# A hybrid attention layer on one core: every attention stage gets its own place in the order, and the second attention's values take one matmul per key block

## The chip, the cores and the metric

The kernel runs on one core of one Trainium2 chip. Its engines work side by side, each through its own queue: TensorE (PE; its weight loads are listed as PEld) multiplies matrices into banks of PSUM, VectorE (DVE) and ScalarE (ACT) work element by element, GpSimd (POOL) does a few scalings, and SyncE (SP) issues most transfers. An engine takes its instructions in their order, and one that waits holds up all that stand behind it. The metric is the time of one execution in microseconds; lower is better.

## The reference

One decoder layer on 256 tokens of width 1024, in 32-bit floats. The normalised input is multiplied by one wide matrix, and the result is cut into the inputs of three mixers and their gates:

```python
h = rmsnorm(x, g_in);  z = h @ w_in
(mq, mk, mv, mg, dq, dk, dv, dg, iq, ik, iw, xq, xg, glog) = split(z)
ya = moba_attention(rope(mq), rope(mk), mv)              # 8 heads of 64
yb = dsa_attention(rope(dq), rope(dk), dv, rope(iq), rope(ik), iw)   # 8 heads, the 64 best keys each
yc = cross_attention(xq, *split(rmsnorm(mem, g_mem) @ w_mem_kv))     # 4 heads of 128, 256 memory rows
u  = sum over b of sigmoid(glog_b + b_merge_b) * ((y_b * silu(gate_b)) @ w_up_b)
out = rmsnorm(x + u @ w_out, g_final)
```

With 256 tokens the first attention (m) has one block, its own, and is plain causal attention. The second (d) adds a selection mask: an indexer scores all keys for each query from iq, ik and iw, and the 64 best stay.

## The kernel before

**Precision in halves.** A matrix product of 32-bit numbers is taken as three products of rounded parts: a number is split into hi (rounded) and lo (the rest), and hi·hi, hi·lo and lo·hi are added up in PSUM. So each weight piece (w0, w1, … in the order of use) is loaded raw (w5r), cast to hi on ScalarE (w5h, L253) and subtracted to lo on VectorE (w5l, L255), two operations of 128x1024 for most pieces, and then used by TensorE three times. The token activations (x) and the memory rows (e) are split the same way once.

**Steps.** The program is a list of numbered steps, each one weight piece; a step has two halves of 12 matmuls for most products. ORDER gives the sequence of the products: mq, mk, i (the indexer), dq, dk, xq (cross queries), xk and xv (cross keys and values), the gates mg, dg and xg, then l (the merge gates' logits), u (the up projections) and at the end the output. Everything else is attached by step number: `at(25.5, f)` runs f between the two halves of step 25, `at(26, f)` before its first half. Weights are loaded six steps ahead and split three steps ahead.

**Who sets the order.** TensorE and GpSimd run in the order in which the program is written, that is, by these steps. The order on VectorE, ScalarE and SyncE is set by the framework's scheduler from when it thinks operands are ready; LO_BEHIND pins one weight's subtraction behind one value split.

**Attention stages.** One block of the first or second attention is a pair of heads. `scores` puts both heads' scores (msc or dsc, six matmuls a head) into one PSUM bank each, tag "sc", of which there are two. VectorE reduces each with mask and maximum (L608, shown as CUSTOM_DVE and a read of its accumulator), ScalarE takes the exponentials with their sums (L612), VectorE the reciprocal (L620), GpSimd scales (mpr, dpr, L622), TensorE transposes (mtp, dtp, one bank, tag "tp", L633), ScalarE casts hi (L634), VectorE subtracts lo (mpl, dpl, L635), TensorE multiplies by the values (mya, dya, L648), and ScalarE and VectorE bring the result out (L653, L654). A value operand carries hi and lo of v side by side in its 128 columns, so that rows 0 to 63 of the product are hi and 64 to 127 lo. Four matmuls make a head: probabilities hi and lo, for each of two key blocks (256 and 128 query columns). They go into one half of the bank of tag "y" (there is one), the pair of heads shares the bank, and one copy (ScalarE) and one add (VectorE) bring a head out.

The indexer's queries and keys are rotated (the rope products, L408 to L412), split (iqs, iks), transposed through the "sc" banks (iqt, L459) and the "tp" bank (ikt, L463); its heads' scores (lg, L486) take "sc" banks too. The cross attention takes "sc" for its scores (xsc) and "y" for its values (xya). mBt (L919) spreads the memory rows' scale m_rstd.

M_PAIRS, D_PAIRS and X_HEADS give two steps for each pair or head, from which `attend` derives the other stages by fixed distances.

Of the kernel before, what the change touches and what calls it, by code (L numbers as in the profile page):

```python
# [68 lines left out]
)  # L69
# [43 lines left out]
def hybrid_layer_kernel(  # L113
# [144 lines left out]
    def product(ps, a, b, first, last):  # L258
        (ah, al), (bh, bl) = a, b
        nc.tensor.matmul(ps, ah, bh, start=first, stop=False)  # L260
# [1 line left out]
        nc.tensor.matmul(ps, al, bh, start=False, stop=last)  # L262
# [812 lines left out]
```

## Time and profile before

| | us |
|---|---|
| time, median of 3 runs | 323.35 (322.94 to 323.82) |
| span of the profiled execution | 321.2 |
| TensorE busy | 313.0 (97%) |
| TensorE weight loads busy | 298.2 (93%) |
| VectorE busy | 252.1 (78%) |
| ScalarE busy | 202.4 (63%) |
| GpSimd busy | 42.1 (13%) |
| TensorE clock granted, mean | 0.994 |

The profiled execution shows its span, from its first to its last instruction, and no time of its own beside it; 323.35 − 321.2 = 2.15 us is what lies around the span if it ran like the median. Busy time is a share of the span; matmuls overlap in the pipeline, so a busy TensorE may still be running at less than its best. The chain that ended last is followed back from the last instruction, and shows which engine had to be faster for the end to come earlier. A row of the timeline gives start, duration, engine, line, operation and operands (out<-in); what a row waited for is in brackets.

### The profile page before, as it was taken

The numbers are of one execution on the slowest core, as the hardware profiler recorded it, in microseconds if no ns is written. First come the engines' busy times: TensorE is split into PE (matmuls) and PEld (weight loads), VectorE is DVE, ScalarE is ACT, GpSimd is POOL, SyncE is SP. The second block draws the span as 40 slices with busy tenths as digits, with TensorE's granted clock in tenths as the row PEclk, the third lists the DMA queues.
The fourth block names the chain that finished last, engine by engine and source line by source line (L and its number), as shares of the span: only waits on it lengthen the run. The fifth ranks groups of instructions, "written<-read, shape, count | busy, mean of one in ns | idle before, by whom it ended". The sixth has DMA issues, their size and how long they took to land.

```text
span 321.2 us, 6394 instructions
## 1 busy us (share of the span) xinstructions
PE 313.0 (97%) x2442; PEld 298.2 (93%) x2442; DVE 252.1 (78%) x458; ACT 202.4 (63%) x357; POOL 42.1 (13%) x58
## 2 busy tenths in 40 slices
PE   8999999999999999999999999999999999999992
PEld 7899999998999989889999999999999999998882
DVE  3579999999799999988866669999466866677533
ACT  5599665687877636477666688755454546653434
POOL 0001000017202000020200235411000111014011
PEclk9999999999999999999999999999999999999997
DMA  7999886965545346484444434488756666656003
GB/s 214 376 334 326 267 264 183 282 222 138 191 131 141 126 137 229 158 254 138 134 133 131 135 130 133 134 261 271 221 178 193 192 192 198 185 157 187 2 0 131
DMA packets 18367, 59.45 MB, mean 185 GB/s; under 512 B 2208, under 2 KB 2464, under 8 KB 18336
## 3 DMA queue, kind: packets, MB, share of 16 engines
q1 hardware_dynamic: 17760, 57.73, 57.3%
q10 hardware_dynamic: 576, 1.31, 1.1%
q8 instruction: 19, 0.31, 0.4%
q14 instruction: 12, 0.10, 0.1%
HBM read 55.89 MB, written 1.05 MB: 177 GB/s over the span
## 4 chain that ended last, share of the span: by engine, by line
PE 83%; ACT 5%; DVE 5%; DMA 3%; issue 2%; SPq 0%; ACTq 0%; DVEq 0%
DMA w3r<-w_in 2%; PE i_0ps L286 2%; PE i_1ps L286 2%; PE xv_0ps L286 2%; PE dv_0ps L286 2%; PE xv_1ps L286 2%; PE dv_1ps L286 2%; PE lg L486 1%; PE o_0ps L261 1%; PE o_0ps L262 1%; PE o_0ps L260 1%; DMA w0r<-w_in 1%; ACT mpr L612 1%; PE dya L648 1%; PE mv_1ps L286 1%
## 5 line engine op out<-in xcount | busy, mean ns | idle before, releaser
L753 POOL TENSOR_TENSOR u<-u,gt 128x512 f32<-128x512 f32 x7 | 9.9, 1413 | 76.7 <-DVE gt L750 76.7
L622 POOL TENSOR_SCALAR dpr<-dpr,dst 128x128 f32<-128x128 f32 (+1 forms) x16 | 6.6, 426 | 83.4 <-DVE dst L620 83.2
L622 POOL TENSOR_SCALAR mpr<-mpr,mst 128x128 f32<-128x128 f32 (+1 forms) x16 | 9.8, 628 | 56.0 <-DVE mst L620 56.0
L740 ACT ACTIVATE gt<-gt,x_first 128x256 f32<-128x256 f32 x24 | 10.9, 501 | 3.7 <-DVE gt L737 3.6
L612 ACT ACTIVATE dpr<-dms,dst 128x128 f32<-128x128 f32 (+1 forms) x16 | 7.1, 445 | 3.6 <-DVE dst L608 3.6
L612 ACT ACTIVATE mpr<-mms,mst 128x128 f32<-128x128 f32 (+1 forms) x16 | 7.1, 445 | 2.1 <-DVE mst L608 2.1
L794 ACT ACTIVATE junk<-xn 128x512 f32<-128x512 f32 (+1 forms) x5 | 2.7, 543 | 8.6 <-DVE xn L792 8.6
L670 ACT ACTIVATE xpr<-xsc,xst,xs_rstd 128x256 f32<-128x256 f32 x8 | 4.5, 560 | 4.1 <-DVE xst L666 4.1
L758 ACT CAST us<-u 128x512 fp32r<-128x512 f32 x4 | 2.5, 623 | 6.2 <-POOL u L753 4.9
L490 ACT ACTIVATE rl<-lg 128x384 f32<-128x384 f32 x8 | 3.9, 486 | 2.7 <-PE lg L486 1.6
L653 ACT COPY dyT<-dya 64x256 f32<-64x256 f32 x8 | 2.9, 368 | 4.2 <-PE dya L648 4.0
L493 DVE SCALAR_TENSOR_TENSOR acc<-rl,iw,acc 128x128 f32<-128x128 f32 (+1 forms) x14 | 5.4, 433 | 0.1
L974 PE MATMUL warm<-ones 128*128 128x128 f32 x18 | 4.2, 430 | 1.1 <-DVE eps_t L969 1.1
L486 PE MATMUL lg<-ikT,iqT 128*128 128x128 f32 (+1 forms) x32 | 5.1, 281 | 0.1
L608 DVE CUSTOM_DVE_ANT_0 mms<-msc,bias_c 128x128 f32<-128x128 f32 (+1 forms) x16 | 5.0, 348 | 0.0
L974 PEld LDWEIGHTS warm<-ones 128*128 128x128 f32 x18 | 3.9, 330 | 1.0 <-DVE eps_t L969 1.0
L635 DVE TENSOR_TENSOR dpl<-dtp,dph 128x384 fp32r<-128x384 f32 x8 | 4.4, 555 | 0.4
L654 DVE TENSOR_TENSOR dyT<-dyT,dya 64x256 f32<-64x256 f32 x8 | 3.3, 418 | 1.8 <-ACT dyT L653 1.7
L608 DVE CUSTOM_DVE_ANT_0 dms<-dsc,sel 128x128 f32<-128x128 f32 (+1 forms) x16 | 4.7, 353 | 0.0
L634 ACT CAST dph<-dtp 128x384 fp32r<-128x384 f32 x8 | 3.8, 479 | 1.4 <-PE dtp L633 1.3
L504 DVE MATCH_REPLACE8 wk<-m,wk 128x128 f32<-128x128 f32 (+1 forms) x14 | 4.7, 345 | 0.0
L792 DVE TENSOR_TENSOR xn<-o_0ps,xn 128x512 f32<-128x512 f32 x2 | 1.4, 692 | 4.2 <-PE o_0ps L262 4.2
(1296 smaller groups left out, 1544.3 us busy)
## 6 DMA issues: line engine op xcount, KB each, us to landing
x_rows<-x SPq DMA_DIRECT2D x2, 512.0 KB, 8.9
eT<-memT SPq DMA_DIRECT2D x4, 256.0 KB, 4.6
xn<-x SPq DMA_DIRECT2D x2, 512.0 KB, 4.8
w0r<-w_in SPq DMA_DIRECT2D x2, 256.0 KB, 3.3
w1r<-w_in SPq DMA_DIRECT2D x2, 256.0 KB, 4.3
xT<-xT SPq DMA_DIRECT2D x2, 256.0 KB, 6.6
w2r<-w_in SPq DMA_DIRECT2D x1, 512.0 KB, 6.7
w3r<-w_in ACTq DMA_DIRECT2D x1, 512.0 KB, 7.8
```

Source lines behind the costliest of these rows:

```text
L286: nc.tensor.matmul(accs[nm][t][:, :n], a[p](k, slice(t * P, (t + 1) * P)), w[q][:, half, :], start=k + i == 0, stop=k + i == nk + 1,)
L486: nc.tensor.matmul(lg[:, c : c + n], q[:, q0:q1], idx["k"][:, j, 0:n], start=j == 0, stop=j == 1)
L493: nc.vector.scalar_tensor_tensor(acc[:, c], rl[:, c], iw[:, t, g : g + 1], (bias_c if g == 0 else acc)[:, c], op0=OP.mult, op1=OP.add,)
L504: nc.vector.match_replace(out=wk[:, c], in_to_replace=m8[t], in_values=src[:, c], imm_value=TAKEN)
L608: nc.vector.tensor_tensor_reduce(out=ms[:, c], in0=sc[:, c], in1=bias()[:, c], op0=OP.add, op1=OP.min, scale=-(HD**-0.5), scalar=3e38, acc ...
L612: big["last_exp"] = nc.scalar.activation(pr[:, c], ms[:, c], AF.Exp, bias=st[:, t : t + 1], scale=-1.0, accum_out=st[:, 2 + t : 3 + t],)
L622: nc.gpsimd.tensor_scalar(pr[:, c], pr[:, c], st[:, 4 + t : 5 + t], 1.0, op0=OP.mult, op1=OP.mult)
L635: marks[f"{nm}pl{hd}"] = nc.vector.tensor_sub(pl, tp[:, 0 : 3 * P], ph.bitcast(F32)).ins
L670: big["last_exp"] = nc.scalar.activation(pr3[:, t, :], sc[:, t, :], AF.Exp, bias=st[:, t : t + 1], scale=xs_rstd[:, t : t + 1], accum_out= ...
L740: nc.scalar.activation(gt[:, f, :], gt[:, f, :], AF.Sigmoid, bias=x_first[:, j : j + 1])
L753: adder.tensor_tensor(u, u, gt, op=OP.add)
L974: nc.tensor.matmul(warm[:, 0:P], ones, ones, start=True, stop=True)
```

## The change

1. **Places.** The tables of pairs become one table per stage (scores, scales, turns, values), with an entry for every block or head, and the indexer's turn and heads, the ropes, and the memory rows get places of their own. ORDER is permuted. LO_BEHIND is empty.
2. **Second attention's values (APART).** hi and lo of a head's probabilities lie side by side in one tile; a head takes two matmuls, one per key block, with both halves as moving operand (512 columns, then two times 128 columns). Each head fills a whole "y" bank: [hi·hi and hi·lo | lo·hi and lo·lo]. One ScalarE copy and two VectorE adds bring three of these four quarters out.
3. **Shared banks.** The two column halves of mq, and of xk, share one PSUM bank; their evacuation is one operation where it was two. The indexer's keys are transposed into one tile and copied once.
4. **Tiles.** The reduction writes straight into the probabilities' tile (no ms); six such tiles in place of four.

SC, MM, SQ_ONE, EARLY and the branch for two blocks at once are new names whose values leave the work as it was.

```diff
-ORDER = (
-    "mk0", "mk1", "i0", "dq0", "xq0", "i1", "dq1", "dk0", "dk1", "xk0", "xq1", "dv", "xk1",
-    "xv", "mg0", "mg1", "dg0", "dg1", "xg0", "xg1", "l10", "l01", "l00", "u00", "l02", "u10",
-    "l20", "l03", "u01", "u02", "l21", "u03", "u20", "l11", "u11", "l22", "l23", "u21", "l12",
-    "l13", "u12", "u13", "u23", "u22",
-)
+ORDER = ('mk0', 'mk1', 'i0', 'xq0', 'dq0', 'i1', 'dq1', 'dk0', 'xq1', 'dk1', 'xk0', 'dv', 'xk1',
+         'xv', 'mg0', 'mg1', 'xg1', 'dg1', 'dg0', 'l01', 'xg0', 'l00', 'l10', 'u00', 'l02', 'u10',
+         'l20', 'l03', 'u01', 'u03', 'u20', 'l21', 'u02', 'l22', 'l11', 'l12', 'l23', 'u11', 'u21',
+         'l13', 'u12', 'u13', 'u23', 'u22')
...
-IDX = (27, 29, 33.5)
-TURNS = (('mq', 8.5, 15.5), ('mk', 13.5, 20.5), ('dq', 27, 30), ('dk', 34, 37.5))
-M_PAIRS = ((23, 25.5), (24, 27.5), (26.5, 29.5), (29.5, 31.5))
-D_PAIRS = ((43.5, 47.5), (47.5, 49), (52, 53.5), (54.5, 55.5))
-X_HEADS = ((41.5, 44), (44.5, 46.5), (49, 51), (50.5, 52.5))
+IDX_TURN = (27, 28, 28)
+IDX_HEADS = (29, 30.0, 30.0, 31.0, 31, 31.5, 32, 32.5)
+IDX_TOP = 33.5
+TURNS = (('mq', 8.5, 15.0), ('mk', 14.5, 20.5), ('dq', 28.0, 32.5), ('dk', 34, 35.5))
...
+M_BLOCKS = (1, 1, 1, 1)
+M_SCORES = (23, 25.5, 26.0, 29.5)
+M_SCALES = (23.5, 24.5, 27.0, 26.0, 27.0, 27.0, 30.0, 31.0)
+M_TURNS = (25.5, 26.5, 27.5, 28.5, 29.5, 30.5, 31.5, 33.5)
+M_VALUES = (26.5, 27.5, 28.5, 29.5, 30.5, 32.5, 34.0, 36.0)
+D_BLOCKS = (1, 1, 1, 1)
+D_SCORES = (43.5, 47.5, 52, 54.5)
+D_SCALES = (44, 44.5, 48, 48.5, 52.5, 53.5, 55, 56.5)
+D_TURNS = (45.5, 47.5, 49, 50, 53.5, 55.0, 56.0, 57.0)
+D_VALUES = (48.5, 49.0, 50, 51, 54.5, 56.0, 57.0, 61.0)
+X_SCORES = (41.5, 44.0, 48.5, 48.0)
+X_SCALES = (42, 45, 49.0, 51)
+X_TURNS = (44, 46.5, 51.0, 52.0)
+X_VALUES = (45.5, 48, 53.0, 53.5)
+MEM_ROWS = 23.5
+APART = ('d',)
 GATES = 59.5
-LO_BEHIND = {29: "mpl0"}
-MEM = (2, 7, 11, 15, 21.5)
+LO_BEHIND = {}
+MEM = (2, 3, 10, 15, 19.5)
...
+    def pair_bank(nm):
+        return acc_bank(nm).rearrange("p (f s) -> p f s", f=2)
...
+    def products_t(ps, w, act, ks, nk, cols, f=None):
...
-                (a[0](k, slice(0, S)), a[1](k, slice(0, S))), k == 0, k == nk - 1,
+                (a[0](k, slice(0, S)), a[1](k, slice(0, S))), k == 0 and not f, k == nk - 1,
+                f is not None,
...
-        tp = psum.tile([P, 2, S], F32R, name=f"ikt{t}", tag="tp", bufs=1)
-        for j in range(2):
-            nc.tensor.transpose(tp[:, j, 0:P], idx["ks", t][:, j, :], ident_r)
-        nc.vector.tensor_copy(idx["k"][:, :, tok], tp[:, :, 0:P])
+
+    def idx_keys():
+        tp = psum.tile([P, 2, S], F32R, name="ikt", tag="tp", bufs=1)
+        for u in range(2):
+            for j in range(2):
+                nc.tensor.transpose(tp[:, j, u * P : u * P + P], idx["ks", u][:, j, :], ident_r)
+        nc.vector.tensor_copy(idx["k"], tp)
...
-        for f in range(2):
-            nc.vector.tensor_tensor(sk[:, f, :], accs[f"xk{hf}"][f], mB, op=OP.mult)
+        nc.vector.tensor_tensor(sk, accs[f"xk{hf}"], pair_rows(mB), op=OP.mult)
...
-            ms = work.tile([P, 3 * P], F32, name=f"{nm}ms{hd}", tag="ms")
-            st = work.tile([P, 6], F32, name=f"{nm}st{hd}", tag="st", bufs=4)
-            pr = work.tile([P, 4 * P], F32, name=f"{nm}pr{hd}", tag="pr", bufs=4)
+            st = keep.tile([P, 6], F32, name=f"{nm}st{hd}", tag="st", bufs=6)
+            pr = work.tile([P, 4 * P], F32, name=f"{nm}pr{hd}", tag="pr", bufs=6)
...
-                    out=ms[:, c], in0=sc[:, c], in1=bias()[:, c], op0=OP.add, op1=OP.min,
+                    out=pr[:, c], in0=sc, in1=bias()[:, c], op0=OP.add, op1=OP.min,
...
     def self_values(nm, hd):
...
+        if nm in APART:
+            ya = psum.tile([P, 2, S], F32, name=f"{nm}ya{hd}", tag="y", bufs=1)
+            both = big[nm, "pt", hd]
+            nc.tensor.matmul(ya, v[:, 0, hd, :, :], both[:, :, 0:S], start=True, stop=False)
+            nc.tensor.matmul(
+                ya[:, :, P:S], v[:, 1, hd, :, :], both[:, :, S : 3 * P], start=False, stop=True
+            )
+            high, low = ya[0:HD], ya[HD:P]
+            if e:
+                first = keep.tile([P, S], F32, name=f"{nm}yf{hd}", tag="yf")[0:HD]
+                nc.scalar.copy(first, high[:, 0, :])
+                nc.vector.tensor_tensor(y, first, high[:, 1, :], op=OP.add)
+                nc.vector.tensor_tensor(y, y, low[:, 0, :], op=OP.add)
+            else:
+                nc.scalar.copy(y, low[:, 0, :])
+                for i in range(2):
+                    nc.vector.tensor_tensor(y, y, high[:, i, :], op=OP.add)
+            return
```

The first place is VectorE around the second score block of the first attention (mms or mpr on the left; msc_965 and msc_966 are its two heads before, msc_1008 and msc_1009 with the change; ISA is the masked reduction and the read of its accumulator). Before:

```order
L608 ISA mms_979,mst_980<-msc_965,bias_c 128x128
L608 ISA mst_980 128x1
L412 TENSOR_TENSOR ik_948<-ik1t_949,ik1t_950 128x64
L442 TENSOR_TENSOR iqs_954<-iq_648,iqs_954 128x8x64
L608 ISA mms_979,mst_980<-msc_965,bias_c 128x256
L608 ISA mst_980 128x1
L444 TENSOR_TENSOR iks_955<-ik_948,iks_955 128x64
L608 ISA mms_986,mst_987<-msc_966,bias_c 128x128
L608 ISA mst_987 128x1
L608 ISA mms_986,mst_987<-msc_966,bias_c 128x256
L608 ISA mst_987 128x1
L255 TENSOR_TENSOR w28l<-w28r,w28h 128x1024
```

and with the change:

```order
L656 RECIPROCAL mst_887<-mst_887 128x2
L275 TENSOR_TENSOR w28l<-w28r,w28h 128x1024
L437 TENSOR_TENSOR ik_942<-ik1t_943,ik1t_944 128x64
L467 TENSOR_TENSOR iqs_948<-iq_648,iqs_948 128x8x64
L469 TENSOR_TENSOR iks_949<-ik_942,iks_949 128x64
L644 ISA mpr_1023,mst_1022<-msc_1008,bias_c 128x128
L644 ISA mst_1022 128x1
L644 ISA mpr_1023,mst_1022<-msc_1008,bias_c 128x256
L644 ISA mst_1022 128x1
L644 ISA mpr_1029,mst_1028<-msc_1009,bias_c 128x128
L644 ISA mst_1028 128x1
L644 ISA mpr_1029,mst_1028<-msc_1009,bias_c 128x256
```

The weight split w28l and the rotated indexer halves (iqs, iks) now stand ahead of both reductions, where before the reductions stood between them and ahead of w28l. On TensorE the third block's scores come 12 product matmuls and one transposition behind the second's, where before 60 product matmuls, two transpositions and a head's values lay between.

The second place is TensorE at the first head of the second attention's values. Before:

```order
L648 MATMUL dya_2199<-dph_2118,dv 128x256
L648 MATMUL dya_2199<-dpl_2119,dv 128x256
L648 MATMUL dya_2199<-dph_2118,dv 128x128
L648 MATMUL dya_2199<-dpl_2119,dv 128x128
L633 MATMUL dtp_2208<-cst,dpr_1940 128x128 x3
L260 MATMUL dg0ps<-xhi,w48h 128x256
```

and with the change:

```order
L684 MATMUL dya_2188<-dpt_2009,dv 128x512
L685 MATMUL dya_2188<-dpt_2009,dv 128x2x128
L280 MATMUL xsc_2197<-xkh,xqT 128x256
L281 MATMUL xsc_2197<-xkl,xqT 128x256
L282 MATMUL xsc_2197<-xkh,xqT 128x256
L280 MATMUL xsc_2197<-xkh,xqT 128x256
L281 MATMUL xsc_2197<-xkl,xqT 128x256
L282 MATMUL xsc_2197<-xkh,xqT 128x256
```

Two matmuls stand for four, the second one with two strided pieces of 128 columns, and a head of cross scores now follows; 12 product matmuls later comes the second head.

The third place is VectorE at the same head (dyT is the result, dyf the odd heads' first quarter, xst the cross scores' maximum). Before:

```order
L709 COPY yxT<-xya_2169 128x256
L255 TENSOR_TENSOR w52l<-w52r,w52h 128x1024
L654 TENSOR_TENSOR dyT<-dyT,dya_2199 64x256
L635 TENSOR_TENSOR dpl_2207<-dtp_2208,dph_2206 128x384
L255 TENSOR_TENSOR w53l<-w53r,w53h 128x1024
L635 TENSOR_TENSOR dpl_2230<-dtp_2231,dph_2229 128x384
L665 TENSOR_REDUCE xst_2244<-xsc_2237 128x2
L666 TENSOR_TENSOR xst_2244<-xst_2244,xs_rstd 128x2
L654 TENSOR_TENSOR dyT<-dyT,dya_2199 64x256
```

and with the change:

```order
L719 TENSOR_REDUCE xst_2160<-xsc_2153 128x2
L275 TENSOR_TENSOR w52l<-w52r,w52h 128x1024
L720 TENSOR_TENSOR xst_2160<-xst_2160,xs_rstd 128x2
L697 TENSOR_TENSOR dyT<-dyT,dya_2188 64x256
L719 TENSOR_REDUCE xst_2204<-xsc_2197 128x2
L697 TENSOR_TENSOR dyT<-dyT,dya_2188 64x256
L720 TENSOR_TENSOR xst_2204<-xst_2204,xs_rstd 128x2
L732 RECIPROCAL xst_2160<-xst_2160 128x2
L732 RECIPROCAL xst_2204<-xst_2204 128x2
L692 TENSOR_TENSOR dyT<-dyf_2225,dya_2222 64x256
```

Each head has two adds, and the maximum of the next cross head stands between those of the first.

More of the change, by code (lines that the diff above doesn't have):

```diff
@@ L207, in row_sums @@
         ps = psum.tile([P, 512], F32, name=f"{nm}ss", tag="tp", bufs=1)
+        sq = acts[nm, "sq"]
+        if SQ_ONE:
+            nc.vector.tensor_tensor(sq[:, 0, :], sq[:, 0, :], sq[:, 1, :], op=OP.add)
         for t in range(2):
-            for j in range(2):
+            for j in range(2 - SQ_ONE):
                 nc.tensor.matmul(
-                    ps[:, t : t + 1], acts[nm, "sq"][:, j, t * P : (t + 1) * P], ones[:, 0:1],
-                    start=j == 0, stop=j == 1,
+                    ps[:, t : t + 1], sq[:, j, t * P : (t + 1) * P], ones[:, 0:1],
+                    start=j == 0, stop=SQ_ONE or j == 1,
                 )
@@ L456, in idx_transpose @@
         for j in range(2):
-            tp = psum.tile([P, 4, P], F32R, name=f"iqt{t}{j}", tag="sc", bufs=2)
+            tp = psum.tile([P, 4, P], F32R, name=f"iqt{t}{j}", tag="sc", bufs=SC)
             for g in range(4):
@@ L481, in idx_head @@
     def idx_head(g):
[L482 removed]
+        lg = psum.tile([P, 512], F32, name=f"lg{g}", tag="sc", bufs=SC)
         q = idx["q"][g // 4][:, g % 4, :]
@@ L488, in idx_head @@
                 )
-        rl = work.tile([P, 3 * P], F32, name=f"rl{g}", tag="ms")
+        rl = work.tile([P, 4 * P], F32, name=f"rl{g}", tag="pr", bufs=6)[:, 0 : 3 * P]
         nc.scalar.activation(rl, lg[:, : 3 * P], AF.Relu, scale=HD**-0.5)
@@ L499, in idx_round @@
         src, wk = idx["acc" if r == 0 else "wk"], idx["wk"]
-        m8 = [work.tile([P, 8], F32, name=f"m8_{r}{t}", tag="m8", bufs=4) for t in range(2)]
+        m8 = [
+            work.tile([P, 16], F32, name=f"m8_{r}{t}", tag="m8", bufs=4)[:, 0:8] for t in range(2)
+        ]
         for t, c in PARTS:
@@ L627, in self_transpose @@
         pr, _ = prs.pop((nm, hd))
-        ph, pl = prs[nm, "t", hd] = [
-            work.tile([P, 3 * P], F32R, name=f"{nm}p{p}{hd}", tag=f"pt{p}") for p in "hl"
-        ]
+        both = big[nm, "pt", hd] = work.tile([P, 2, 3 * P], F32R, name=f"{nm}pt{hd}", tag="pt")
+        ph, pl = prs[nm, "t", hd] = both[:, 0], both[:, 1]
         tp = psum.tile([P, 512], F32, name=f"{nm}tp{hd}", tag="tp", bufs=1)
@@ L650, in self_values @@
                 )
-        own, other = (slice(HD * i, HD * i + HD) for i in (e, 1 - e))
-        y = big[nm + "y"][own, b, :]
         nc.scalar.copy(y, ya[other, :])
@@ L658, in cross_scores @@
     def cross_scores(hd):
-        sc = psum.tile([P, 2, S], F32, name=f"xsc{hd}", tag="sc", bufs=2)
+        sc = psum.tile([P, 2, S], F32, name=f"xsc{hd}", tag="sc", bufs=SC)
         kT = [p[:, hd, :] for p in big["xk"]]
@@ L878, in hybrid_layer_kernel, with attend @@
     at(end["dv"], v_evac, "dv")
[L880 to L889 removed]
+    def attend(nm, blocks, starts, scales, turns, values, bias):
+        for g, s0 in enumerate(starts):
+            at(s0, self_scores, nm, sum(blocks[:g]), blocks[g], bias)
+        for hd in range(NH):
+            at(scales[hd], self_scale, nm, hd)
+            at(turns[hd], self_transpose, nm, hd)
+            at(values[hd], self_values, nm, hd)
+    attend("m", M_BLOCKS, M_SCORES, M_SCALES, M_TURNS, M_VALUES, lambda: bias_c)
+    attend("d", D_BLOCKS, D_SCORES, D_SCALES, D_TURNS, D_VALUES, lambda: idx["sel"])
     x_rows = []
```

138 lines of the change are left out of this document (70 added, 68 removed).

## The prediction

> **What bounds the kernel now.** I read the page first, then the chain, the waits of TensorE, the windows, and last the timeline of TensorE in the windows that are not full.
>
> ```profile
> span 321.2 us, 6394 instructions
> PE 313.0 (97%) x2442; PEld 298.2 (93%) x2442; DVE 252.1 (78%) x458; ACT 202.4 (63%) x357; POOL 42.1 (13%) x58
> ...
> PE 83%; ACT 5%; DVE 5%; DMA 3%; issue 2%; SPq 0%; ACTq 0%; DVEq 0%
> ```
>
> TensorE is busy for 313.0 of 321.2 us and the chain runs through it for 83% of the span. So an edit is worth what it takes from TensorE's own instructions, or from the few places where TensorE waits. The windows (PE, PEld, DVE, ACT, POOL, then clock, DMA, GB/s) show where these are:
>
> ```profile
> 60.00:70.00 10.00, 9.96 (x84) 9.07 (x83) 9.97 (x30) 8.99 (x17) 0.83 (x2) 1.00 0.83 266
> 70.00:80.00 10.00, 9.64 (x83) 8.80 (x82) 9.84 (x34) 7.08 (x21) 6.42 (x10) 1.00 0.51 143
> 80.00:90.00 10.00, 9.76 (x87) 9.62 (x87) 7.68 (x13) 7.93 (x18) 1.65 (x4) 1.00 0.62 184
> 90.00:100.00 10.00, 9.88 (x89) 9.37 (x88) 9.48 (x24) 8.28 (x21) 1.82 (x4) 1.00 0.36 109
> ...
> 190.00:200.00 10.00, 9.88 (x85) 9.68 (x84) 9.06 (x15) 8.54 (x16) 5.36 (x3) 1.00 0.49 152
> ```
>
> TensorE has gaps between 60 and 100 us and around 192 us. In 60 to 80 us VectorE is full (9.97 and 9.84 of 10), so anything that TensorE wants from VectorE there stands in a queue with no slack. The granted clock is 1.00 in all of these windows. The waits view and the starts on TensorE give the sizes (start, duration, line, operation):
>
> ```profile
> PE iqt L459 <- DVE mst L608: 0.4, 1, 0.4
> PE mq_0ps L262 <- DVE w3l L255: 0.2, 1, 0.2
> PE ikt L463 <- DVE mpl L635: 0.2, 1, 0.2
> ```
>
> ```profile
> 65.50 0.31 PE L286 MATMUL i_1ps<-w23h,xlo 128*128 128x320 f32 x1
> 65.85 0.40 PE L919 MATMUL mBt<-cst,m_rstd 128*128 128x128 f32 x2
> ...
> 67.06 0.33 PE L476 MATMUL msc<-mkhi,mqhi 64*128 64x128 f32 x2
> ...
> 67.95 0.39 PE L260 MATMUL dq1ps<-xhi,w24h 128*128 128x256 f32 x1
> ...
> 75.44 0.28 PE L648 MATMUL mya<-mph,mv 128*128 128x256 f32 x1
> 75.71 0.39 PE L648 MATMUL mya<-mpl,mv 128*128 128x256 f32 x1
> ...
> 77.90 0.28 PE L260 MATMUL dk0ps<-xhi,w26h 128*128 128x256 f32 x1
> ...
> 78.83 0.28 PE L262 MATMUL dk0ps<-xhi,w26l 128*128 128x256 f32 x1
> 79.47 1.10 PE L459 MATMUL iqt<-ident_r,iqs 128*128 128x128 f32 x8 [0.36 <-DVE mst L608]
> ...
> 84.22 0.80 PE L459 MATMUL iqt<-ident_r,iqs 128*128 128x128 f32 x8
> 85.23 0.36 PE L463 MATMUL ikt<-ident_r,iks 128*128 128x128 f32 x2 [0.21 <-DVE mpl L635]
> ...
> 94.53 0.28 PE L262 MATMUL dk1ps<-xhi,w29l 128*128 128x256 f32 x1
> 94.93 0.73 PE L486 MATMUL lg<-ikT,iqT 128*128 128x128 f32 x4
> ...
> 191.51 0.28 PE L648 MATMUL dya<-dph,dv 128*128 128x256 f32 x1
> 191.91 0.39 PE L648 MATMUL dya<-dpl,dv 128*128 128x256 f32 x1
> ```
>
> Durations overlap, so a wait shows in the starts. From 77.90 to 78.83 eight matmuls of 256 columns go by: 0.116 us each, the undisturbed pace. A start that comes later than that has waited. mBt comes 0.35 us after a 320-column matmul whose like take 0.15: 0.20 lost. The second mya matmul is 0.27 behind the first: 0.15 lost. The first iqt is 0.64 behind the last dk0: 0.52 lost; and the eight iqt take 1.10 there against 0.80 at 84.22, so 0.3 more inside them. ikt starts 0.2 after the end of iqt (85.02), where a transpose's start normally comes 0.2 before that end: 0.4 lost. lg is 0.40 behind dk1: 0.28 lost. The last dya is 0.40 behind: 0.28 lost. The sum is 2.1 us. The span of 321.2 lies 2.15 under the median of 323.35; I add that 2.15 to every span that I work out.
>
> **The change part by part: waits removed.** ikt moves into one tile behind both iqt pairs, and the wait for the bank "tp" with it, since the value split that it waited for now ends before. The memory row sums go two steps earlier (19.5 for 21.5), so the statistic that mBt reads is ready before it: its four small VectorE steps no longer lie between the score reductions. iqt no longer comes right behind a score block: 24 matmuls of 0.116 and the values of a head lie between them, 2.8 us, against reductions of 1.1 us. lg, mya and the last dya are pulled apart from their producers in the same way (dya by one step and more). I take all six as gone, −2.1; the bound on the other side is that mya and lg and half of the iqt wait come back elsewhere, −1.3.
>
> **A wait added: third score block of the first attention.** Its step moves from 26.5 to 26.0 and the second one's from 24 to 25.5, so that the third needs both "sc" banks 12 matmuls and one transposition after the second block has filled them. VectorE must empty them, and the reductions stand behind a long queue there (the order quoted with the change):
>
> ```profile
> 67.84 0.40 DVE L408 TENSOR_TENSOR i10t<-i_0ps,tab 128x256 f32<-128x256 f32 x1
> ...
> 70.03 0.68 DVE L442 TENSOR_TENSOR iqs<-iq,iqs 128x512 fp32r<-128x512 f32 x1
> 70.63 0.22 DVE L444 TENSOR_TENSOR iks<-ik,iks 128x64 fp32r<-128x64 f32 x1
> ...
> 73.11 0.28 DVE L608 CUSTOM_DVE_ANT_0 mms<-msc,bias_c 128x128 f32<-128x128 f32 x1
> ...
> 73.66 1.24 DVE L255 TENSOR_TENSOR w28l<-w28r,w28h 128x1024 fp32r<-128x1024 f32 x1
> ```
>
> TensorE: dq1 begins where the second block began, at 67.06 less the 0.20 of mBt, 66.85. 36 matmuls of 0.116 bring it to 71.05, the block takes 0.89 (67.06 to 67.95), the three transposes 0.27 (rows below, 158.97 to 159.24), 12 matmuls 1.39: the third block is due at 73.6. VectorE: from the first rope product (67.84) to the end of w28l (73.66 and 1.24, 74.9) it did in 7.1 us just the work that now lies ahead of the bank's release, both reductions of 0.55 (73.11 to 73.66) among it. It can begin when the index product ends, 67.1 (66.85 and 0.3 of drain), so the second bank is free at 74.2, and up to 0.3 later if w28l, now ahead of the second iqs, holds that back. The wait is 0.6 to 0.9; I take **0.7**. Its bounds: 0, since an idle VectorE would need only 1.1 for both heads against 1.7 between the blocks, and 1.8, if a second weight split of 1.2 gets in the way. Behind the waiting matmul on TensorE stands everything, so it counts in full.
>
> Smaller waits: ikt's copy, two index heads that follow the fourth block, and the first handover of second values (next paragraph) are due within 0.3 us of what they wait for, by the same kind of count. I take 0.1 each, **0.3**; bounds 0 and 0.8.
>
> **Second attention's values.** The rows of one head before, with those of a 512-column matmul and of the evacuation:
>
> ```profile
> 128.82 0.40 PE L286 MATMUL xv_1ps<-w40h,ehi 128*128 128x512 f32 x1
> 129.05 0.40 PE L286 MATMUL xv_0ps<-w40l,ehi 128*128 128x512 f32 x1
> ...
> 158.56 0.28 PE L648 MATMUL dya<-dph,dv 128*128 128x256 f32 x1
> ...
> 158.97 0.51 PE L633 MATMUL dtp<-cst,dpr 128*128 128x128 f32 x3
> 159.24 0.36 PE L260 MATMUL dg0ps<-xhi,w48h 128*128 128x256 f32 x1
> ```
>
> ```profile
> 159.17 0.37 ACT L653 COPY dyT<-dya 64x256 f32<-64x256 f32 x1 [0.86 <-PE dya L648]
> ...
> 159.57 0.41 DVE L654 TENSOR_TENSOR dyT<-dyT,dya 64x256 f32<-64x256 f32 x1
> ...
> 163.50 0.68 DVE L665 TENSOR_REDUCE xst<-xsc 128x2 f32<-128x512 f32 x1
> ```
>
> Four matmuls took 0.41 us (158.56 to 158.97) for 768 columns. The two new ones move the same 768: 0.23 (128.82 to 129.05) and 0.116, 0.35 together. Eight heads save 8 × 0.06 = **0.5**. The bounds are 0, if the two strided halves of 128 columns run as slowly as two matmuls, and 0.9, if the removed pair saves two full steps of 0.06 a head.
>
> The Trainium skill, "TensorE: Matmul & The Clock Gate", section "LDWEIGHTS (loading the stationary operand)", puts a load of 128 columns at about 107 ns whatever the rows. By that rule four loads pace a head at 0.43 us, which the 0.41 of the row bears out; two matmuls would take 0.34, and the saving would be 0.7 in place of 0.5.
>
> The price is on VectorE: a second add per head, 8 × 0.41 = 3.3 us, at 150 to 200 us. In 190 to 200 VectorE has 0.9 us to spare; the adds of the first four heads lie earlier. They cost nothing unless the bank is late, for the "y" bank now holds one head, and each head's matmuls wait until the last has been copied and added twice. The tightest handover is from the first to the second head: 6 matmuls of scores and 12 of the gate product, 18 × 0.116 = 2.1 us and the second value matmul's own 0.1. The drain (0.3), the copy (0.37), two adds (0.8) and the maximum that stands between them (0.68) make 2.15. This is the handover that I counted at 0.1.
>
> The shared banks of mq and xk, the one scaling in place of two, the direct write of the reduction and the moved loads act on ScalarE, VectorE and the queues. What covers them is the stock of split weights: the only one that TensorE waited for in the whole span is w3l, 0.2 us in the first 20. I cost them at nothing. If the cover were gone, one piece late by one split would cost 1.2 (w28l). The new order of products and the tail hold the same matmuls, and cost nothing as long as their banks are free.
>
> **The sum.** −2.1 + 0.7 + 0.3 − 0.5 = −1.6: a span of 319.6, and with 2.15 a time of **321.8**. By the bounds: −2.1 − 0.9 = −3.0, 320.3; and −1.3 + 1.8 + 0.8 = +1.3, 324.6.
>
> **The rivals.** *Waits only move* (no change): the third block waits the full 1.8 and the small ones 0.5 together, and the merge gives 0.3: −2.1 + 1.8 + 0.5 − 0.3 = −0.1, 323.3. For it: VectorE's 9.97 and 9.84. Against it: up to 100 us the change puts nothing more into VectorE's queue, it only reorders it.
>
> *Slower: the single bank of second values.* In each of the three close handovers (heads 0 to 3) a weight cast on ScalarE or a weight split on VectorE (1.2) gets in front of the copy or an add. I count 0 to 0.5 of slack there, so each costs about 0.9; and the first head waits as long for the cross-attention values, which use the same bank. Four times 0.9 is 3.6; with the 0.1 already counted taken out, −1.6 + 3.5 = +1.9, 325.3. It decides from 0.7 a handover, where the sum passes +1. For it: exponentials and a cast stand ahead of these copies on ScalarE. Against it: the copy before came at once (159.17, 0.2 after TensorE had gone on to the next operation), and ScalarE has a third of its time free.
>
> *All waits gone:* the third block's banks are free in time and a head saves 0.1: −2.1 + 0.3 − 0.9 = −2.7, 320.6.
>
> *The merge does nothing:* two narrow halves cost two loads; −1.1, 322.2.
>
> **How the numbers follow.** My forecast 0.47, waits only move 0.16, slower 0.15, all gone 0.12, merge does nothing 0.10. About 0.3%, 1 us, can be told from no change, so 322.4 and 324.3 are the limits. Faster: 0.44 of the forecast, 0.12, and half of the last, 0.61; no change: 0.03, 0.16 and 0.05, 0.24; slower 0.15. The range 320.2 to 324.1 leaves out the slow case and a little below.
>
> **What would show it.** The waits of TensorE after should name no iqt, ikt or mBt, and a new one of 0.6 to 0.9 at the third msc block near 73.6 us, released by VectorE's reductions. dya should show 0.35 us from its start to the next matmul. Windows 80:90 and 90:100 should be full, 70:80 at about 9.3 to 9.6. I am wrong if the msc wait is over 1.8 or under 0.2, if dya rows carry waits of 0.5 and more, or if the product order brings new waits beyond 200 us.

## The result

The changed kernel takes 321.40 us (median of 6 runs, 320.93 to 322.27) against 323.18 (322.66 to 323.82) for the kernel before beside it: a ratio of 0.9945, 95% interval 0.9928 to 0.9963, 1.8 us less. In a second set of runs (e10 below) it was 321.54 against 323.25, ratio 0.9960 (0.9945 to 0.9975). Forecast were 321.8 and 1.6 us. Ratios leave out an execution that takes over 1.5% more than the fastest of its kernel, and so do the times given for e1 and e6, which have one such each.

The page and the waits view of the profile after:

```profile
span 319.8 us, 6334 instructions
PE 311.6 (97%) x2426; PEld 297.3 (93%) x2426; DVE 252.3 (79%) x463; ACT 201.6 (63%) x355; POOL 41.7 (13%) x58
```

```profile
PE warm L1029 <- DVE eps_t L1024: 1.1, 1, 1.1
PE msc L519 <- DVE mst L644: 0.5, 2, 0.3
PE mv_0ps L309 <- ACT w2h L273: 0.2, 1, 0.2
PE mq0ps L282 <- DVE w1l L275: 0.2, 1, 0.2
```

iqt and ikt are gone from the list, and msc, waiting for VectorE's reductions, has come in; the two last rows lie in the first 13 us. TensorE has 16 matmuls less and VectorE 5 operations more. The windows that had gaps (columns as in the prediction):

```profile
70.00:80.00 10.00, 9.46 (x87) 8.71 (x86) 9.78 (x38) 8.80 (x25) 5.10 (x12) 1.00 0.40 117
80.00:90.00 10.00, 10.00 (x94) 10.00 (x93) 8.16 (x13) 7.92 (x16) 1.68 (x5) 1.00 0.71 189
90.00:100.00 10.00, 10.00 (x91) 9.72 (x91) 9.77 (x26) 8.36 (x21) 1.62 (x4) 1.00 0.29 95
...
190.00:200.00 10.00, 10.00 (x88) 9.95 (x87) 9.68 (x14) 7.80 (x13) 3.03 (x2) 1.00 0.45 127
```

All are full but 70 to 80, the place of the new wait. TensorE's timeline there, and at the first two heads of the second attention's values:

```profile
74.52 0.27 PE L282 MATMUL dq1ps<-xhi,w25l 128*128 128x256 f32 x1
75.10 0.32 PE L519 MATMUL msc<-mkhi,mqhi 64*128 64x128 f32 x1 [0.31 <-DVE mst L644]
75.66 0.32 PE L519 MATMUL msc<-mkhi,mqhi 64*128 64x128 f32 x1 [0.23 <-DVE mst L644]
...
76.54 0.39 PE L280 MATMUL dk0ps<-xhi,w26h 128*128 128x256 f32 x1
...
159.37 0.39 PE L684 MATMUL dya<-dpt,dv 128*128 128x512 f32 x1
159.60 0.28 PE L685 MATMUL dya<-dpt,dv 128*128 128x256 f32 x1
159.72 0.28 PE L280 MATMUL xsc<-xkh,xqT 128*128 128x256 f32 x1
...
161.70 0.28 PE L282 MATMUL xg1ps<-xhi,w48l 128*128 128x256 f32 x1
161.84 0.47 PE L684 MATMUL dya<-dpt,dv 128*128 128x512 f32 x1
162.15 0.28 PE L685 MATMUL dya<-dpt,dv 128*128 128x256 f32 x1
```

The third score block starts 0.58 us behind the last product matmul, where the second block, which did not wait, started 0.21 behind its own: 0.37 lost. The first score of the block's second head then comes 0.56 later, where the two go side by side when nothing waits. From the product ahead of the block to the operation behind it 2.02 us pass (74.52 to 76.54); at the second block it was 1.10 (71.74 to 72.84), so 0.92 is lost in all. A head of values takes 0.35 (159.37 to 159.72). The second head of values starts 0.14 behind the product, against 0.116 without a wait, and its own second matmul comes 0.31 later (162.15) where the first head's came 0.23 later: the tight handover cost 0.11. VectorE shows why the block waited:

```profile
67.44 0.28 DVE L644 CUSTOM_DVE_ANT_0 mpr<-msc,bias_c 128x128 f32<-128x128 f32 x1
...
68.88 0.41 DVE L433 TENSOR_TENSOR i10t<-i_0ps,tab 128x256 f32<-128x256 f32 x1
...
72.41 1.20 DVE L275 TENSOR_TENSOR w28l<-w28r,w28h 128x1024 fp32r<-128x1024 f32 x1
73.53 0.22 DVE L437 TENSOR_TENSOR ik<-ik1t,ik1t 128x64 f32<-128x64 f32 x1
73.67 0.68 DVE L467 TENSOR_TENSOR iqs<-iq,iqs 128x512 fp32r<-128x512 f32 x1
74.27 0.22 DVE L469 TENSOR_TENSOR iks<-ik,iks 128x64 fp32r<-128x64 f32 x1
74.41 0.28 DVE L644 CUSTOM_DVE_ANT_0 mpr<-msc,bias_c 128x128 f32<-128x128 f32 x1
...
74.96 0.28 DVE L644 CUSTOM_DVE_ANT_0 mpr<-msc,bias_c 128x128 f32<-128x128 f32 x1
...
75.52 0.08 DVE L644 DVE_READ_ACCUMULATOR2_ANT mst<- 128x1 f32 x1
```

The scores of the second block were there at about 73.0; VectorE came to them at 74.41, after the weight split and the rotated halves, without an idle moment.

To see where the time went, the span can be cut at the first matmuls of some products (starts on TensorE, us between them; each column is one execution):

| stretch | before | change | e10 | e3 | e4 | e5 | e7 |
|---|---|---|---|---|---|---|---|
| first mv to first mk (the head) | 24.20 | 24.90 | 24.85 | 24.79 | 24.44 | 25.61 | 25.64 |
| first i to first dv | 71.27 | 70.01 | 69.39 | 69.32 | 71.55 | 71.52 | 71.54 |
| first dv to first mg0 | 30.13 | 31.43 | 31.43 | 31.43 | 30.13 | 30.13 | 30.91 |
| first mg0 to first u00 | 66.61 | 64.68 | 64.70 | 64.68 | 68.60 | 66.82 | 64.68 |
| first u00 to first o | 84.00 | 84.00 | 84.00 | 84.00 | 84.00 | 84.80 | 84.00 |

Some work moved between the middle rows (a head of cross scores and late value heads now come before mg0), so they are added up: from i to u00 168.0 before, 166.1 with the change, 165.5 in its second trace. With the change one head of the first attention's values, 0.4 us, stands behind the first dv. Counted back, the stretch up to dv gained 0.85 and 1.5 us in the two traces, and the stretch from dv to u00 1.05 in both. The head differs by 1.8 us between e5 and e11 (23.83), whose programs differ only further on, so nothing is read from it.

### The profile page after: what moved, and what is told of

Its sections match the earlier page's. It is cut to its first block, busy times and chain, and to the rows that moved or that the text cites. A ratio compares the mean times of both kernels' runs of the same rounds, so it can differ in the third digit from the quotient of the medians.

```text
span 319.8 us, 6334 instructions
## 1 busy us (share of the span) xinstructions
PE 311.6 (97%) x2426; PEld 297.3 (93%) x2426; DVE 252.3 (79%) x463; ACT 201.6 (63%) x355; POOL 41.7 (13%) x58
## 3 DMA queue, kind: packets, MB, share of 16 engines
HBM read 55.89 MB, written 1.05 MB: 178 GB/s over the span
## 4 chain that ended last, share of the span: by engine, by line
PE 74%; DVE 10%; DMA 6%; ACT 4%; issue 4%; SPq 0%; ACTq 0%; DVEq 0%
DMA w3r<-w_in 3%; PE xv_0ps L309 2%; PE dv_0ps L309 2%; PE xv_1ps L309 2%; PE dv_1ps L309 2%; DMA w26r<-w_in 2%; DMA w0r<-w_in 1%; PE o_0ps L282 1%; PE o_0ps L281 1%; PE o_0ps L280 1%; PE lg L530 1%; PE dsc L519 1%; PE mya L704 1%; DVE elo L205 1%; DMA w15r<-w_in 1%
## 5 line engine op out<-in xcount | busy, mean ns | idle before, releaser
L807 POOL TENSOR_TENSOR u<-u,gt 128x512 f32<-128x512 f32 x7 | 13.4, 1911 | 66.5 <-DVE gt L804 51.4
L648 ACT ACTIVATE dpr<-dpr,dst 128x128 f32<-128x128 f32 (+1 forms) x16 | 7.2, 450 | 5.5 <-DVE dst L644 5.5
L648 ACT ACTIVATE mpr<-mpr,mst 128x128 f32<-128x128 f32 (+1 forms) x16 | 7.1, 449 | 1.1 <-DVE mst L644 1.1
L204 ACT ACTIVATE ehi<-eT,x_first 128x256 fp32r<-128x256 f32 x8 | 3.6, 502 | 4.5 <-DMA eT<-memT 4.5
L644 DVE CUSTOM_DVE_ANT_0 dpr<-dsc,sel 128x128 f32<-128x128 f32 (+1 forms) x16 | 4.8, 355 | 0.3 <-PE dsc L519 0.2
L781 POOL TENSOR_TENSOR dgzn<-dgzn,dyT 128x512 f32<-128x512 f32 x2 | 3.3, 1661 | 11.9 <-DVE dyT L693 6.2
L670 DVE TENSOR_TENSOR dpt<-dtp,dpt 128x384 fp32r<-128x384 f32 x8 | 4.4, 553 | 0.6 <-ACT dpt L669 0.3
L704 PE MATMUL mya<-mpt,mv 128*128 128x256 f32 (+1 forms) x32 | 4.7, 271 | 0.0
L644 DVE CUSTOM_DVE_ANT_0 mpr<-msc,bias_c 128x128 f32<-128x128 f32 (+1 forms) x16 | 4.7, 349 | 0.0
L704 PEld LDWEIGHTS mya<-mpt,mv 128*128 128x128 f32 x32 | 4.5, 188 | 0.2
```

Source lines behind the costliest of these rows:

```text
L644: nc.vector.tensor_tensor_reduce(out=pr[:, c], in0=sc, in1=bias()[:, c], op0=OP.add, op1=OP.min, scale=-(HD**-0.5), scalar=3e38, accum_out ...
L648: big["last_exp"] = nc.scalar.activation(pr[:, c], pr[:, c], AF.Exp, bias=st[:, t : t + 1], scale=-1.0, accum_out=st[:, 2 + t : 3 + t],)
L670: marks[f"{nm}pl{hd}"] = nc.vector.tensor_sub(pl, tp[:, 0 : 3 * P], ph.bitcast(F32)).ins
L704: nc.tensor.matmul(ya[:, o], v[:, k, hd, :, :], p[:, c], start=k + i == 0, stop=k + i == 2)
L807: adder.tensor_tensor(u, u, gt, op=OP.add)
```

## The experiments

**The wait at the third score block: e2 and e3.** In e2 the second block comes earlier, with VectorE's order unchanged; in e3 the third comes later, with one weight split pinned.

```diff
-M_SCORES = (23, 25.5, 26.0, 29.5)
+M_SCORES = (23, 25, 26.0, 29.5)          # e2
+M_SCORES = (23, 25.5, 26.5, 29.5)        # e3
-LO_BEHIND = {}
+LO_BEHIND = {30: "mpl1"}                 # e3
```

> The changed kernel with the first attention's second score block 12 matmuls earlier (25 in place of 25.5). VectorE's order is the same, so both reductions still stand behind the weight split and the rotated halves; the third block is due at the same time. Theory (VectorE's queue sets the wait): the wait of 0.8 us at the third block stays, 321.4. Rival (the two blocks are too close together, and the reductions need the time from the scores' end): with 1.4 us more between them the wait is gone, 320.6.

> The changed kernel with the third score block 12 matmuls later (26.5 in place of 26.0), and one weight split (w30l) pinned behind the second head's value split so that VectorE's order stays as it was. Theory: the block is due 1.4 us later, more than the 0.8 that it waited; the indexer's transposes come 2.0 us after it and need 1.4, so nothing new waits: 320.6. Rival (the wait moves to the indexer's transposes or to the values of the first heads): 321.4.

e2: 322.24 us, ratio 0.9955 (0.9934 to 0.9977), no different from the change. Its timeline has the second block at 71.34 and the third still waiting:

```profile
71.34 0.33 PE L519 MATMUL msc<-mkhi,mqhi 64*128 64x128 f32 x2
...
75.97 0.32 PE L519 MATMUL msc<-mkhi,mqhi 64*128 64x128 f32 x1 [0.33 <-DVE mst L644]
76.53 0.33 PE L519 MATMUL msc<-mkhi,mqhi 64*128 64x128 f32 x1 [0.23 <-DVE mst L644]
```

The wait has the same size, 0.93 by the starts, with 1.4 us more between the blocks. VectorE's operations stand in the same order as in the change and follow each other without a gap. So the distance is not the cause; VectorE's queue is.

e3: 321.35 us, ratio 0.9935 (0.9917 to 0.9954). The wait at the block is gone, and half of it has turned up at the indexer's keys:

```profile
75.78 0.33 PE L519 MATMUL msc<-mkhi,mqhi 64*128 64x128 f32 x2
...
84.31 0.53 PE L491 MATMUL ikt<-ident_r,iks 128*128 128x128 f32 x4 [0.31 <-DVE mpt L670]
```

From i to dv it is 69.32, where the change had 70.01 and 69.39. The theory's 0.8 was not won: it is 0.1 to 0.7 by the traces, and the times cannot tell it from the change.

**Chasing the wait further: e9, beside e10, the change once more.** e9 is e3 with one more weight split pinned.

```diff
-LO_BEHIND = {30: "mpl1"}
+LO_BEHIND = {30: "mpl1", 31: "mpl2"}
```

> As e3 (third score block 12 matmuls later, w30l pinned), and w31l pinned behind the third head's value split too. In e3 the indexer's keys still waited 0.44 us for the bank that this value split frees, and the split stood behind w31l. Theory (VectorE's queue order sets this wait too): it goes, 0.4 us less than e3: 320.9, 0.5 below the changed kernel. Rival (the weight split then comes late for TensorE, or the wait moves on to the index heads): 321.4.

> The changed kernel itself, beside e9 on one chip, and as a second trace of it: 321.4 by its first runs; the head (to the first key matmul) was 24.9 us, the stretch from the first up projection to the output 84.00 us.

e9 took 321.86 us, ratio 0.9960 (0.9942 to 0.9978), e10 321.54, ratio 0.9960. The rival was right: ikt no longer waits, but its copy now holds up the next transposition.

```profile
86.66 0.55 PE L668 MATMUL mtp<-cst,mpr 128*128 128x128 f32 x3 [0.45 <-DVE ikT L492]
```

From i to dv its trace takes 70.43 us, more than that of the change. In the change VectorE is busy for 9.78, 8.16 and 9.77 of 10 between 70 and 100 us, and in these two attempts a release that was brought forward delayed another. No version tried beats the change by more than can be measured. In e10 the wait at the third block was 0.56 in place of 0.92: it is not the same in every execution.

**The merge without its places: e4, e5, e11.** These have the places and the order of products of the kernel before. e5 also has the four value matmuls of before, so that only the shared banks, single evacuations and tiles are left of the change; e11 is e5 with the halves of the probabilities in two tiles again; e4 has the two merged matmuls.

```diff
-APART = ('d',)
+APART = ()                               # e5 and e11; e4 keeps ('d',)
+M_PAIRS = ((23, 25.5), (24, 27.5), (26.5, 29.5), (29.5, 31.5))
+D_PAIRS = ((43.5, 47.5), (47.5, 49), (52, 53.5), (54.5, 55.5))
...
-        both = big[nm, "pt", hd] = work.tile([P, 2, 3 * P], F32R, name=f"{nm}pt{hd}", tag="pt")
-        ph, pl = prs[nm, "t", hd] = both[:, 0], both[:, 1]
+        ph, pl = prs[nm, "t", hd] = [    # e11
+            work.tile([P, 3 * P], F32R, name=f"{nm}p{p}{hd}", tag=f"pt{p}") for p in "hl"
+        ]
```

> The changed kernel's code (two matmuls a head of second values, shared banks) with all places and the order of products of the kernel before. Theory (places and merge add up): the waits of before come back, the third block's wait goes, so only the merge's 0.5 is left: 322.7. Rival (the single bank of values needs the new places): at the old ones, a head a step, the second add makes waits of 0.3 or more in four or five handovers, 323.2 or more.

> The changed kernel's code with all places, the order of products and the four value matmuls of the kernel before: of the change only the shared banks, the single evacuations, the one copy of the indexer's keys and the direct write of the reduction are left. Theory (these cost and save nothing on the path): within 0.3% of the kernel before, and its waits. Then the 2.1 us by which the merge at the old places lost is the merge's own. Rival (the shared banks come free later and carry part of those 2.1 us): 324.5 or more.

> As e5 (shared banks, old places, four matmuls; 2.0 us slower than the kernel before), but the halves hi and lo of the probabilities in two tiles again, as before. In e5 the 720 matmuls from the first up projection to the output took 84.80 us, in every merged kernel and in the kernel before 84.00, with nothing waiting. Theory (the one tile's placement puts TensorE into the slower rhythm): 84.00 again, and 0.8 to 1.1 us less than e5. Rival (the rhythm has another cause): 84.80 and e5's time.

e4: 325.70 us, ratio 1.0073 (1.0053 to 1.0092), so slower than before. Three handovers of the one bank wait:

```profile
165.74 0.47 PE L679 MATMUL dya<-dpt,dv 128*128 128x512 f32 x1 [0.25 <-DVE dyT L688]
...
193.08 0.47 PE L679 MATMUL dya<-dpt,dv 128*128 128x512 f32 x1 [1.02 <-DVE dyT L688]
...
197.88 0.47 PE L679 MATMUL dya<-dpt,dv 128*128 128x512 f32 x1 [1.05 <-DVE dyT L692]
```

By their starts 0.41, 1.18 and 1.21 us are lost, 2.8 together. This is the prediction's slow rival, at the old places: the merge saves its part and the single bank takes back more (68.60 from mg0 to u00, where e5 has 66.82). Ahead of the second of these waits the copy on ScalarE stood behind the load of an activation table (189.26, 1.28 us) and a gate's activation; ahead of the third, the adds stood behind a weight split and a gate's scaling on VectorE:

```profile
193.58 2.32 DVE L270 TENSOR_TENSOR w60l<-w60r,w60h 128x1024 fp32r<-128x1024 f32 x1
...
196.53 0.40 DVE L692 TENSOR_TENSOR dyT<-dyT,dya 64x256 f32<-64x256 f32 x1
```

e5: 325.06 us, ratio 1.0054 (1.0038 to 1.0070); e11: 324.27, ratio 1.0031 (1.0019 to 1.0042). Neither theory holds. The shared banks and tiles are not free by themselves: 1 to 2 us. Of this 0.8 stands in a stretch in which TensorE waits for nothing. The windows view, 210 to 290 us, of the kernel before and of e5:

```profile
210.00:290.00 80.00, 80.00 (x688) 80.00 (x688) 57.66 (x57) 43.71 (x57) 6.57 (x6) 1.00 0.69 209
```

```profile
210.00:290.00 80.00, 80.00 (x681) 80.00 (x681) 55.81 (x55) 42.28 (x55) 9.07 (x6) 1.00 0.66 205
```

At the same clock and fully busy, e5 gets 681 matmuls through where the kernel before gets 688. e11 has the same 84.80 us from u00 to o, so the one tile is not the reason, though its time is 0.8 us below e5's. Which part of the banks and tiles it is stays open. Outside this stretch both traces lose 0.5 us more from i to u00 (168.47 and 168.48 against 168.0), and the rest of what separates e5 from e11 lies in the head.

**The merge's places: e7.** e4 with the second and the cross attention at their new places, the old order of products and the old first attention.

```diff
-D_PAIRS = ((43.5, 47.5), (47.5, 49), (52, 53.5), (54.5, 55.5))
-X_SCORES = (41.5, 44.5, 49, 50.5)
+D_SCORES = (43.5, 47.5, 52, 54.5)
+D_VALUES = (48.5, 49.0, 50, 51, 54.5, 56.0, 57.0, 61.0)
+X_SCORES = (41.5, 44.0, 48.5, 48.0)
...
```

> As e4 (merged values, places and order of products of the kernel before), but the second attention and the cross attention at their new places. Theory (the merge needs these places, since one bank a head must be emptied by three operations before the next): the three waits of e4 at dya, 2.8 us, go, 325.7 falls to 322.9, about 0.5 below the kernel before. Rival (the waits come from the order of the gate products, which is still the old one): 324.5 or more with dya still waiting.

322.19 us, ratio 0.9964 (0.9951 to 0.9978), a little better than the theory's 322.9. No dya waits, and from mg0 to u00 it has the change's 64.68. The waits at mBt, mya, iqt, ikt and lg are all still there, 1.9 us together. So the places of the second attention carry e4 from 1.0073 to 0.9964, 3.5 us. By the times two thirds or more of the change's gain is there without the first attention's places. By the traces it is less: from i to u00 e7 gains 0.9 us on the kernel before, where the change gains 1.9 and 2.5.

**Four matmuls at the new places: e1 and e6.** e1 is the change with the four value matmuls; e6 also pins one weight split.

```diff
-APART = ('d',)
+APART = ()                               # e1 and e6
-LO_BEHIND = {}
+LO_BEHIND = {60: "dy5"}                  # e6: w60l behind the sixth head's add
...
```

> The changed kernel, but the second attention's values as before: four matmuls a head, a half bank a head, one copy and one add. Theory (the merge saves TensorE time): 0.06 us a head at the matmuls and a little at the transposition behind them, 8 heads, so 0.5 to 0.6 us slower than the changed kernel's 321.4, about 321.9. Rival 1 (two strided halves cost as much as two matmuls): 321.4. Rival 2 (the second add and the single bank cost more than the merge saves): 321.0 or less, with no wait at the second head of values.

> The changed kernel with four value matmuls (e1), and the weight split w60l pinned behind the sixth head's add, which stood behind it and held TensorE up for 1.7 us before the seventh head. Theory (that one idle stretch also brought the 3.2 us at half clock behind it): both go, 1.5 + 1.75 us, 327.3 falls to 324.0; what stays above the changed kernel is the merge's 0.6 and four waits of 0.3 to 0.4. Rival (the half clock has another cause): 325.8, with the low clock still in the trace.

e1: 326.51 us, ratio 1.0109 (1.0079 to 1.0138), over 4 us above the theory. VectorE's scheduler has put the sixth head's add behind a weight split and a gate's scaling, and the seventh head, which needs the bank, waits for it. TensorE, VectorE, and the windows behind it (the clock is the column before the last two):

```profile
193.79 0.27 PE L282 MATMUL xg0ps<-xhi,w56l 128*128 128x256 f32 x1
195.48 1.06 PE L704 MATMUL dya<-dpt,dv 128*128 128x256 f32 x4 [1.41 <-DVE dyT L708]
...
198.02 0.41 PE L281 MATMUL xg0ps<-xlo,w57h 128*128 128x256 f32 x1
198.24 0.41 PE L282 MATMUL xg0ps<-xhi,w57l 128*128 128x256 f32 x1
```

```profile
193.06 1.22 DVE L275 TENSOR_TENSOR w60l<-w60r,w60h 128x1024 fp32r<-128x1024 f32 x1
194.19 0.69 DVE L769 TENSOR_TENSOR dgzn<-dg1ps,rB 128x512 f32<-128x512 f32 x1
194.91 0.42 DVE L708 TENSOR_TENSOR dyT<-dyT,dya 64x256 f32<-64x256 f32 x1
```

```profile
194.00:196.00 2.00, 0.44 (x3) 0.21 (x2) 1.94 (x5) 1.64 (x3) 1.22 (x1) 1.00 0.24 27
196.00:198.00 2.00, 2.00 (x13) 2.00 (x14) 2.00 (x4) 1.37 (x3) 0.05 (x1) 0.74 0.63 244
198.00:200.00 2.00, 2.00 (x12) 2.00 (x11) 2.00 (x4) 0.63 (x1) 1.01 (x1) 0.50 0.00 0
```

The wait cost 1.6 us, and behind it TensorE ran at half clock until 200.2, a matmul each 0.21 us in place of 0.116, which cost another 1.6. The profiled execution (328.08) and one of 328.50 have mean granted clocks of 0.990 and 0.989, three others of 325.69 to 326.51 have 0.994 to 0.996: it seems that not every execution of e1 has the stretch at half clock. e6 took 325.52 us, ratio 1.0074 (1.0051 to 1.0097): in its trace the wait of 1.6 and the low clock are gone (span 323.7 against 326.3), as the theory has it, but the median fell by 1.0 where over 3 was expected, and the two intervals overlap. The price of the merge can't be read from e1 or e6, since the scheduler's order differs with it: with four matmuls four other heads of e6 lose 0.4 to 0.9 each, and the slow 84.80 comes at the end.

**The first attention's places alone: e8 and e12.** e8 is e5 with the first attention, the indexer, the ropes and the memory rows at their new places; e12 adds one exchange in the order of products.

```diff
+M_SCORES = (23, 25.5, 26.0, 29.5)
+MEM = (2, 3, 10, 15, 19.5)
...
-    "mk0", "mk1", "i0", "dq0", "xq0", "i1",
+    "mk0", "mk1", "i0", "xq0", "dq0", "i1",      # e12
```

> The kernel of e5 (four matmuls, old places) with only the first attention, the indexer, the ropes and the memory rows at their new places. Theory (places of the two attentions add up): the waits at mBt, mya, iqt, ikt and lg go (1.8 us), those at mklo and at the third score block come (1.0 us): 0.8 us faster than e5, ratio to the kernel before about 0.9975. Rival (the old second attention loses what the first gains): 1.0.

> As e8 (four matmuls, first attention at its new places; 2.8 us slower than e5), with xq0 ahead of dq0 in the order of products as in the change. In e8 xq0's evacuation stood ahead of the key rope on VectorE, and the row sums, the first and the third score block waited 0.9, 1.0 and 1.6 us, with a stretch at half clock behind. Theory (these places need this order): the waits fall to the 0.1, 0.2 and 0.8 of the changed kernel and the clock stays: 0.7 below e5, ratio to the kernel before about 1.003. Rival (something else of the new places costs): 1.012 or more.

e8: 327.90 us, ratio 1.0151 (1.0121 to 1.0182), slower even than its rival. The third block loses 1.5 us there, and in this execution the half clock follows again:

```profile
76.91 0.32 PE L518 MATMUL msc<-mkhi,mqhi 64*128 64x128 f32 x1 [0.93 <-DVE mst L643]
77.46 0.33 PE L518 MATMUL msc<-mkhi,mqhi 64*128 64x128 f32 x1 [0.23 <-DVE mst L643]
```

```profile
80.00:82.00 2.00, 2.00 (x12) 2.00 (x12) 1.64 (x3) 1.96 (x9) 0.76 (x3) 0.50 0.86 197
```

e12: 326.37 us, ratio 1.0099 (1.0067 to 1.0131). With xq0 ahead, the waits at the row sums and at the first block all but go, the third block loses 0.65, and from i to dv it takes 70.1 us where e8 took 74.3: the places lean on the order. The time came down by 1.5 only, and the expected 1.003 was missed. A part of it shows in the trace: from mg0 to u00 e12 takes 68.44 us and e8 68.48, where e5, with the same places there, takes 66.82. The 1.6 us are lost at the cross attention's scores, transpositions and values (xsc, xpt and xya). So what the first attention's places win ahead of dv is lost again there. In the change, with the cross attention at its new places, this stretch takes 64.68; why the waits come at the old ones is open. The profiled execution, 324.63, was the quickest of its six; what the others, up to 328.1, lose is not in a trace and stays open too.

## Why the prediction was right

**The waits removed** (−2.1). All six are gone in both traces of the change. Two were larger than counted, since the operation behind the late matmul came late too: from the first matmul of the head to the next operation, the head of mya took 0.67 and that of dya 0.80, where their like take 0.41, so 0.26 and 0.40 in place of 0.15 and 0.28. Up to dv these waits make 2.0 us; with 0.9 or 0.6 taken back at the third block and 0.2 at the first, the gains of 0.85 and 1.5 in that stretch are what remains, give or take 0.3.

**The third score block** (+0.7; 0.6 to 0.9). It lost 0.92 in one trace and 0.56 in the other, just outside this range on either side, for the second block's reductions behind w28l and iqs, as told. The size owes something to luck. The block was due at 73.6 and its bank released at 74.2 by the prediction; in the trace it was 74.7 and 75.6, so 1.1 and 1.4 us later. VectorE began the ropes at 68.88, not at 67.1: it had run the first block's reductions only at 67.44, behind the weight splits w26l and w27l. That this start was 1.8 us off hardly showed in the wait, because TensorE was late as well. e2 shows that the queue, and not the distance, sets it.

**The small waits** (+0.3). The sum held, the places did not: ikt and lg did not wait, the first handover cost the 0.11 that it was counted at, while mklo cost 0.2 at the first block and, in the first trace only, the row sums 0.1. Neither of these two was in the sum.

**The merge** (−0.5). A head went from 0.407 to 0.35, as counted from 768 columns. Two things were missed in the same direction. A transposition behind a head takes 0.245 in place of 0.269: in both kernels one ahead of a product takes 0.245 behind a matmul of 256 columns and 0.27 behind one of 128. Only four of the eight heads have one behind them, so this adds 0.1. And four transpositions that stood right ahead of a score block are no longer there; before, such a one took 0.42 to 0.44 to the first score, where one ahead of a product takes 0.27:

```profile
76.11 0.51 PE L633 MATMUL mtp<-cst,mpr 128*128 128x128 f32 x3
76.55 0.33 PE L476 MATMUL msc<-mkhi,mqhi 64*128 64x128 f32 x2
```

All transpositions of the two attentions together went from 4.95 to 4.17 us on TensorE. About half of the 0.8 comes back elsewhere, since the score blocks now start 0.21 behind a product, where products follow each other at 0.116. From the Trainium skill's rule on weight loads ("TensorE: Matmul & The Clock Gate", "LDWEIGHTS (loading the stationary operand)") 0.7 would have come in place of 0.5. With the transpositions behind the heads the rows give 0.55, between the two.

**Banks and tiles at nothing.** This step was not sound. e5 and e11 put them at 1 to 2 us when they stand without the merge and the new places, 0.8 of it as a slower rhythm of the last products. In the change this rhythm does not appear (84.00 us), as in every kernel run here with merged matmuls, so the total was not hurt; that it was not is luck. The step argued from stocks of weights, and in this stretch TensorE waits for none.

**The slow rival** had the right mechanism: the single bank, its three operations, the handovers. At the places of before it costs 2.8 us (e4), though not at the handovers of heads 0 to 3 that the rival named: most of it is lost ahead of the last two heads. In the change it doesn't cost this, since the heads are spread, and not because VectorE's order is kinder. There too the adds of the seventh head (TensorE 192.17) stand behind a weight split:

```profile
193.01 1.22 DVE L275 TENSOR_TENSOR w60l<-w60r,w60h 128x1024 fp32r<-128x1024 f32 x1
194.15 0.41 DVE L697 TENSOR_TENSOR dyT<-dyT,dya 64x256 f32<-64x256 f32 x1
...
195.86 0.40 DVE L697 TENSOR_TENSOR dyT<-dyT,dya 64x256 f32<-64x256 f32 x1
```

The bank comes free only 4 us behind the head, but the eighth head comes at 204.06 (its place moved from 57.5 to 61). The prediction gave the rival 0.15 and judged it from slack counted by hand; 0.11 at the tightest handover, counted at 0.1, says that this count was good.

**The sum.** −1.6 was forecast, and by the ratios 1.8 and 1.3 were measured. In the two traces the stretch from i to u00 gives 1.9 and 2.5, and the head, which is not in the sum, takes 0.7 back in both; since the head varies that much by itself, the close agreement is in part chance. The 2.15 us that the prediction adds to every span are 1.8 in the runs that list both (319.8 and 321.64 here): the profiled execution before must have been quicker than the median by the rest, and this cancels in the difference. That parts could be added up held for the change as a whole, but not for its parts: merge alone +0.6 us on e5 (their intervals overlap), second places on that −3.5, first places and order on that −0.6 or less by the times. Neither the merge (e4), nor the first places (e8, e12), nor the new places without the merge (e1) is faster than the kernel before.

## What to carry to other kernels

Count each release against its due time in the other engine's queue order: on an engine that is 98% full, as VectorE is here, the wait was set by what stood ahead of the release, and moving the producer (e2) gained nothing. When a buffer is emptied by more operations than before, spread its users in the same edit: the merge lost 2.8 us in waits at the old places and paid at the new. Test parts in combination, since a scheduler that reorders around each edit can make single parts look worse than they are together (e1).
